# First mixer of a two-layer trunk: products of 36 rows padded to 128, mask and identity in float32r, two projections in another pair of PSUM banks

## The chip, the cores and the metric

The kernel runs on one core of a Trainium2 chip, alone. The metric is the device time of one launch in microseconds (us), the median of several runs. The profile is one more execution of the same program, taken with the hardware profiler on.

## The reference, cut to what matters

The reference is a decoder trunk of two layers for one sequence of 512 tokens and 1024 features in float32. Each layer is: half a gated feed-forward network, a mixer, another half feed-forward network, each followed by a layer norm of `alpha*x + sublayer(x)`. The mixer of the first layer has two parts side by side. One is a gated linear recurrence (RG-LRU). The other, which the change touches, is an mLSTM with four heads of width 128:

```python
qk = silu(causal_depthwise_conv(qk, conv_w, conv_b)); q, k = split(qk, 2)
log_f = log_sigmoid(if_pre[..., 4:] + f_bias)
# per head, over all earlier tokens j <= i:
#   weight(i, j) = exp(F_i - F_j + i_j - m_i),  F = cumsum(log_f), m = the running maximum
#   num_i = sum_j (q_i . k_j) weight(i, j) v_j
#   h_i   = num_i / max(|den_i|, exp(-m_i)),  den_i the same sum without v_j
```

The mixer of the second layer (RWKV-7 beside GLA) and the feed-forward networks are not edited.

## The kernel before, in words

**Products.** Activations and weights are split into two float32r parts, a high one and a low one (`xh`/`xl`, `whi`/`wlo`), and a product of the two is three TensorE matmuls: high x high, low x high, high x low (lines 128, 129 and 132, or 152 to 154, or 161 to 163). The high part of a weight is a ScalarE copy (line 99), the low part a VectorE subtraction (line 103). Weights come through two `raw` buffers by DMAs on SyncE's queue (line 87), and go into five `whi` and `wlo` buffers. `weights()` splits two chunks ahead of the one that it returns.

**Order.** The program is written as a sequence; a scheduler with a timeline of its own then sets the order on each engine, and each engine runs its instructions in that order. A small edit can therefore move instructions far from it. On TensorE an instruction that waits holds up all behind it.

**PSUM.** `psum(name, tag)` hands out the eight banks: tag A has four, B and C two each, used in turn. A bank is handed out again when its last reader is done.

**The start.** Line 46 loads the identity matrix `ident` on SyncE's queue, ahead of the four tiles of `x` and the first two weight chunks. `start()` keeps TensorE busy with seven products of zeros (line 63), then `to_xT` (line 174) transposes the first two tiles of `x` with `ident`, ScalarE and VectorE make `xh` (line 166) and `xl` (line 167) of them, and the first feed-forward products begin on the tokens 0 to 255.

**The mixer's front (function `even`, line 314).** After some small loads (`pc`, `ng`, and by lines 331 to 333 a mask of 128x256 numbers, which VectorE casts to bfloat16: an identity and a triangle of -1e30) come the gate projection `p_if` (PSUM tag B) and eight query-key projections, in the order 0, 1, 4, 5, 2, 3, 6, 7 of their tiles. The first four are made in two halves of 256 tokens. Each of the eight takes a bank of tag A; so the fifth to eighth reuse the banks of the first to fourth, once the convolution that reads a bank is done: one ScalarE activation (line 309) and three VectorE operations (line 312). `qk_tile` then applies SiLU (line 373).

**The exponents.** VectorE makes four stretches of F_i - m_i in `Rt` (lines 396 and 398), for key tiles 0 to 3 with 512, 384, 256 and 128 queries. Line 399 copies 32 rows of it to the float32r tile `Rs`, and line 400 puts the rounding rest of the four heads into its rows 32 to 35. `sel` (lines 388 and 389, from `ident`) has the columns that select a head. `pct` (line 405) transposes the per-key terms, and line 407 copies them to `cT`. Per head and key tile, `scores` then does:

- line 416: `pr`, a product over 36 rows of `sel` and `Rs` (tag B): the exponents
- line 417: the mask added to its first 128 columns, a bfloat16 product of identity and triangle
- line 419: the exponential on ScalarE into `wt`
- line 421: `pS`, query x key in plain float32 (tag B too, so `pr` and `pS` alternate on two banks)
- line 423: VectorE multiplies the two into `pT`.

There are 16 such steps. TensorE's part of them is laid among the value projection `pv` (four banks of tag A, lines 152 to 154), the recurrence's projections `prg` and `pgg`, and `po`.

Of the kernel before, what the change touches and what calls it, by code (L numbers as in the profile page):

```python
# [7 lines left out]
F32 = mybir.dt.float32  # L8
F32R = mybir.dt.float32r
BF = mybir.dt.bfloat16  # L10
AF = mybir.ActivationFunctionType
ALU = mybir.AluOpType
P = 128
# [18 lines left out]
class Net:  # L32
    def __init__(self, ctx, tc, a):
        self.tc = tc
        self.nc = nc = tc.nc
        self.a = a
        E = ctx.enter_context
        self.cp = E(tc.tile_pool(name="cp", bufs=1))
        self.wp = E(tc.tile_pool(name="wp", bufs=1))
        self.lp = E(tc.tile_pool(name="lp", bufs=1))  # L40
        self.ps = E(tc.tile_pool(name="ps", bufs=1, space=bass.MemoryType.PSUM))
        self.new_x()
        self.xh = self.cp.tile([P, 8, S], F32R, name="xh")
        self.xl = self.cp.tile([P, 8, S], F32R, name="xl")
        self.ident = self.cp.tile([P, P], F32, name="ident")
        nc.sync.dma_start(self.ident, a["c_ident"])

        self.cp.tile([P, 56], F32, name="pad")
        self.expo = self.cp.tile([P, 1], F32, name="expo")
        nc.gpsimd.memset(self.expo, -0.5)  # L50
        ctx.callback(lambda: self.xp.release())
        self.srcs = []
        self.nl = self.nsp = self.nu = 0
        self.raw = {}
        self.adds = range(0)
        self.spl = {}
# [257 lines left out]
    def even(self, l):  # L314
        nc, a, tc = self.nc, self.a, self.tc
        V, A, T, G = nc.vector, nc.scalar, nc.tensor, nc.gpsimd
        with tc.tile_pool(name="ev", bufs=1) as ep:
            bufs = dict(qk=8, row=4, wt=3, v=4, u=4, rg=6, o=6)

            def slot(tag, n=S):  # L320
                return ep.tile([P, 516 if tag == "v" else S], F32, name=tag, tag=tag, bufs=bufs[tag])[:, :n]
# [5 lines left out]
            IFB = 72  # L327
            ng = ep.tile([P, S], F32, name="ng")
            nc.sync.dma_start(ng, a["ml_norm_g"].broadcast_to([P, S]))
            msk = ep.tile([P, 2, P], BF, name="msk")  # L330
            mtmp = slot("wt", 256)
            nc.sync.dma_start(mtmp.rearrange("p (a b) -> p a b", a=2), a["c_mask_neg"])
            V.tensor_copy(out=msk, in_=mtmp.rearrange("p (a b) -> p a b", a=2))
            wbd = ep.tile([P, 8, P], F32, name="wbd")
            G.memset(wbd, 0.0)
            for i, nm in enumerate(("rg_wa", "rg_wx")):
# [11 lines left out]
            p_qk = {}  # L348
            order = (0, 1, 4, 5, 2, 3, 6, 7)
# [20 lines left out]
            def qk_tile(i):  # L370
                qk[i] = slot("qk")
                self.conv(qk[i], p_qk[i], pc, MCW + i, MCB + i, 8)
                A.activation(qk[i], qk[i], AF.Silu)
# [9 lines left out]

            Rt = ep.tile([32, 1280], F32, name="Rt")
            G.memset(Rt, 0.0)
            Rs = ep.tile([36, 1280], F32R, name="Rs")
            sel = ep.tile([36, 4], F32R, name="sel")
            A.activation(sel[0:32], self.ident[0:32, 0:4], AF.Copy)
            A.activation(sel[32:36], self.ident[32:36, 32:36], AF.Copy)
            R, off = [], 0  # L390
            for bj in range(4):
                n = S - bj * P
# [17 lines left out]
            def scores(h):  # L410
                pT = ep.tile([P, 1280], F32, name=f"pT{h}", tag="pT", bufs=4)
                out, off = [], 0
                for bj in range(4):
                    n = S - bj * P
                    pr = self.psum("pr")
                    T.matmul(pr[:, :n], sel[:, h:h + 1].broadcast_to([36, P]), R[bj], start=True, stop=False)
                    T.matmul(pr[:, :P], msk[:, 0, :], msk[:, 1, :], start=False, stop=True)
                    wt = slot("wt")
                    A.activation(wt[:, :n], pr[:, :n], AF.Exp, bias=cT[:, bj, h:h + 1])
                    pS = self.psum("pS")  # L420
                    T.matmul(pS[:, :n], qk[4 + h][:, bj * P:(bj + 1) * P], qk[h][:, bj * P:], start=True, stop=True)
                    o = pT[:, off:off + n]
                    V.scalar_tensor_tensor(out=o, in0=pS[:, :n], scalar=128 ** -0.5, in1=wt[:, :n], op0=ALU.mult, op1=ALU.mult)
                    out.append(o)
                    off += n
                return out


            for i in order[4:]:
                p_qk[i] = self.psum("pqk", "A")  # L430
                self.project_T(p_qk[i], self.weights())
                qk_tile(i)
            pT = [scores(h) for h in range(4)]

            acc = [self.psum("pv", "A") for _ in range(4)]
# [725 lines left out]
def layouts(inp):  # L1161
    import numpy as np
    c = np.ascontiguousarray
    f = np.float32
# [39 lines left out]
    pc[32:36, 72] = inp["ml_f_bias"][0]  # L1204
    o["ev_pc"] = pc
    o["c_ident"] = np.eye(P, dtype=f)
    mk = np.zeros((P, 2, P), f)
    mk[:, 0] = np.eye(P)
    mk[:, 1] = np.where(np.arange(P)[None, :] < np.arange(P)[:, None], -1e30, 0.0)
    o["c_mask_neg"] = mk  # L1210
    w = inp["od_w_in"][0]
    t = T_chunks(w[:, :1664])
# [62 lines left out]
```

## Time and profile before

| | |
|---|---|
| median of 3 runs | 2037.82 us (2034.89 to 2042.15) |
| the profiled execution's own time | 2032.82 us |
| its span, from the first to the last instruction | 2031.0 us |
| mean granted TensorE clock over the span | 0.992 |
| TensorE busy over the span | 2000.3 us (98%) |
| the mixer's stretch, 380 to 620 us: TensorE busy, granted clock | 237.22 of 240 us, 0.99 |
| the same stretch: VectorE, ScalarE | 172.54 us, 122.58 us |
| second mixer, 1340 to 1640 us: TensorE busy, granted clock | 283.52 of 300 us, 0.96 |

Rows of the timeline give the start in us from the span's start, the duration, the engine (PE is TensorE, PEld its weight loads, DVE VectorE, ACT ScalarE, POOL GpSimd, SP SyncE), the line, the operation with its tiles and shape, and in square brackets the idle time before it and what ended it. Matmuls overlap in these rows: the distance from one start to the next tells what a matmul costs, and its duration does not. A row of a tile or line gives minimum, median and maximum of the duration in ns. A row of DMA issues ends with the us from issue to landing.

### The profile page before, as it was taken

To read this page: it belongs to the slowest core of one execution; us is meant where nothing else is said; L and a number is where in the kernel's file an instruction comes from. 1 tells how busy PE (TensorE), PEld (TensorE's weight loads), DVE (VectorE), ACT (ScalarE), POOL (GpSimd) and SP (SyncE) were. 2 spreads that over 40 slices of the span, in tenths; PEclk is the share of its full clock that TensorE was granted. 3 is DMA by queue.
4 is the path that set the end of the run, shared out by engine and by line. 5 is a ranking of instruction groups with operands and counts; after the bars stand their busy time and mean duration, and the time that the engine had idled before them with its cause. 6 is when DMAs were issued, how large, how long until landed. Compare 5 with 4: busy or idle time off the path is not lost. (4 is left out here: it accounts for less than half of the span.)

```text
span 2031.0 us, 26072 instructions
## 1 busy us (share of the span) xinstructions
PE 2000.3 (98%) x10485; PEld 1660.6 (82%) x10485; DVE 959.9 (47%) x1794; ACT 722.4 (36%) x1272; POOL 101.1 (5%) x162
## 2 busy tenths in 40 slices
PE   9999999999999999999999999999999999999998
PEld 8888888976888888888988888896777788888886
DVE  4332333766784333335533333466756773323335
ACT  4332332456423322331432233158545333322330
POOL 0000000100010000000000000012122210000001
PEclk9999999999999999999999999999998999999999
DMA  5233232332223333331433333254636033333331
GB/s 178 94 96 122 94 101 86 98 93 63 73 85 114 102 94 116 102 94 57 131 94 95 115 102 97 83 163 112 142 67 173 2 97 112 101 96 115 101 96 63
DMA packets 59914, 204.02 MB, mean 100 GB/s; under 512 B 7872, under 2 KB 8336, under 8 KB 59792
## 3 DMA queue, kind: packets, MB, share of 16 engines
q1 hardware_dynamic: 56336, 189.77, 30.0%
q0 software_dynamic: 3456, 12.58, 3.4%
q8 instruction: 82, 1.34, 0.3%
q14 instruction: 40, 0.33, 0.0%
HBM read 198.13 MB, written 4.19 MB: 100 GB/s over the span
## 5 line engine op out<-in xcount | busy, mean ns | idle before, releaser
L99 ACT ACTIVATE whi<-raw 128x512 fp32r<-128x512 f32 x661 | 379.6, 623 | 818.6 <-PE pgu L129 401.7
L103 DVE TENSOR_TENSOR wlo<-raw,whi 128x512 fp32r<-128x512 f32 x610 | 395.0, 687 | 537.6 <-ACT whi L99 511.8
L128 PE MATMUL pgu<-xh,whi 128*128 128x512 f32 (+1 forms) x1568 | 563.4, 368 | 1.6 <-ACT whi L99 1.3
L129 PE MATMUL pgu<-xl,whi 128*128 128x512 f32 (+1 forms) x1568 | 564.5, 368 | 0.0
L132 PE MATMUL pgu<-xh,wlo 128*128 128x512 f32 (+1 forms) x1568 | 353.7, 368 | 0.0
L128 PEld LDWEIGHTS pgu<-xh,whi 128*128 128x128 f32 x1568 | 294.3, 189 | 50.4 <-ACT whi L99 1.5
L129 PEld LDWEIGHTS pgu<-xl,whi 128*128 128x128 f32 x1568 | 295.2, 189 | 48.6
L132 PEld LDWEIGHTS pgu<-xh,wlo 128*128 128x128 f32 x1568 | 275.8, 189 | 48.6
L161 PE MATMUL acc<-whi,hh 128*128 128x512 f32 x704 | 274.6, 390 | 0.0
L162 PE MATMUL acc<-whi,hl 128*128 128x512 f32 x704 | 274.3, 390 | 0.0
L163 PE MATMUL acc<-wlo,hh 128*128 128x512 f32 x704 | 272.5, 390 | 0.0
L239 DVE TENSOR_TENSOR sg<-sg,pgu 128x512 f32<-128x512 f32 (+1 forms) x96 | 61.7, 643 | 335.2 <-PE pgu L132 331.0
L162 PEld LDWEIGHTS acc<-whi,hl 128*128 128x128 f32 x704 | 132.2, 188 | 27.3
L163 PEld LDWEIGHTS acc<-wlo,hh 128*128 128x128 f32 x704 | 132.2, 188 | 27.2
L161 PEld LDWEIGHTS acc<-whi,hh 128*128 128x128 f32 x704 | 132.2, 188 | 27.0
L166 ACT ACTIVATE hh<-sg 128x512 fp32r<-128x512 f32 (+1 forms) x96 | 57.2, 596 | 121.2 <-DVE sg L239 121.2
L196 POOL TENSOR_SCALAR rs<-mv 128x1 f32<-128x1 f32 x24 | 13.1, 547 | 1503.0 <-DVE mv L194 1503.0
L238 ACT ACTIVATE sg<-pgu 128x512 f32<-128x512 f32 (+1 forms) x96 | 53.6, 560 | 55.7 <-PE pgu L132 55.0
L166 ACT ACTIVATE xh<-pst 128x512 fp32r<-128x512 f32 x48 | 27.6, 597 | 112.8 <-PE pst L174 112.6
L128 PE MATMUL pj<-xh,whi 128*128 128x512 f32 (+2 forms) x184 | 61.9, 356 | 0.0
L167 DVE TENSOR_TENSOR hl<-sg,hh 128x512 fp32r<-128x512 f32 (+1 forms) x96 | 61.6, 642 | 0.6 <-ACT hh L166 0.5
L129 PE MATMUL pj<-xl,whi 128*128 128x512 f32 (+2 forms) x184 | 60.5, 346 | 0.0
(346 smaller groups left out, 2006.4 us busy)
## 6 DMA issues: line engine op xcount, KB each, us to landing
raw<-ffn_wi SPq DMA_DIRECT2D x176, 512.0 KB, 3.5
raw<-ffn_wo SPq DMA_DIRECT2D x88, 512.0 KB, 3.5
raw<-od_krv SPq DMA_DIRECT2D x12, 512.0 KB, 3.8
raw<-ev_qk SPq DMA_DIRECT2D x8, 512.0 KB, 3.6
raw<-ev_rg SPq DMA_DIRECT2D x8, 512.0 KB, 3.4
raw<-ev_w_out SPq DMA_DIRECT2D x8, 512.0 KB, 3.5
raw<-od_w_out SPq DMA_DIRECT2D x8, 512.0 KB, 4.0
wlo<-od_krv POOLq DMA_DIRECT2D x6, 512.0 KB, 6.6
```

The costliest lines, as they stand in the source:

```text
L99: self.nc.scalar.activation(hi[:, sl], t[:, sl], AF.Copy)
L103: self.nc.vector.tensor_tensor(out=lo[:, sl], in0=t[:, sl], in1=hi[:, sl].bitcast(F32), op=ALU.subtract)
L128: mm(o, hi[:, kt, :n], self.xh[:, kt, t0:t1], start=kt == 0, stop=False)
L129: mm(o, hi[:, kt, :n], self.xl[:, kt, t0:t1], start=False, stop=lo is None and kt == 7)
L132: mm(o, lo[:, kt, :n], self.xh[:, kt, t0:t1], start=False, stop=kt == 7)
L161: mm(o, ah, hi[:, cs], start=first and i == 0, stop=False)
L162: mm(o, al, hi[:, cs], start=False, stop=False)
L163: mm(o, ah, lo[:, cs], start=False, stop=last and i == len(lhs) - 1)
L166: self.nc.scalar.activation(hi, src, AF.Copy)
L167: self.nc.vector.tensor_tensor(out=lo, in0=src, in1=hi.bitcast(F32), op=ALU.subtract)
L238: nc.scalar.activation(sg, pp[f, 0][:, t0:t1], AF.Silu)
L239: nc.vector.tensor_tensor(out=sg, in0=sg, in1=pp[u][:, t0:t1], op=ALU.mult)
```

## The change

Four edits, and what the scheduler makes of them.

- **Identity.** `ident` becomes a float32r tile (`identr`, read as float32 through `ident`). Its load moves from SyncE's queue to GpSimd's, ahead of the memset of `expo`.
- **Mask.** The mask keeps only its triangle, 128x128, as float32r, and the mask product takes `identr` as its other operand.
- **Rows.** `Rs` and `sel` get 128 rows. Four new ScalarE activations (scale 0 on `expo`) write zeros into their rows 32 to 127; rows 32 to 35 are then overwritten as before. The product of line 416 runs over 128 rows.
- **Banks.** The fifth and sixth query-key projections take the two banks of tag C; the seventh and eighth take the first two of tag A.

```diff
-        self.ident = self.cp.tile([P, P], F32, name="ident")
-        nc.sync.dma_start(self.ident, a["c_ident"])
+        self.identr = self.cp.tile([P, P], F32R, name="ident")
+        nc.gpsimd.dma_start(self.identr, a["c_ident"])
+        self.ident = self.identr.bitcast(F32)
...
-            msk = ep.tile([P, 2, P], BF, name="msk")
-            mtmp = slot("wt", 256)
-            nc.sync.dma_start(mtmp.rearrange("p (a b) -> p a b", a=2), a["c_mask_neg"])
-            V.tensor_copy(out=msk, in_=mtmp.rearrange("p (a b) -> p a b", a=2))
+            msk = ep.tile([P, P], F32R, name="msk")
+            mtmp = slot("wt", P)
+            nc.sync.dma_start(mtmp, a["c_mask_neg"])
+            V.tensor_copy(out=msk, in_=mtmp)
...
-            Rs = ep.tile([36, 1280], F32R, name="Rs")
-            sel = ep.tile([36, 4], F32R, name="sel")
+            Rs = ep.tile([P, 1280], F32R, name="Rs")
+            sel = ep.tile([P, 4], F32R, name="sel")
+
+            A.activation(Rs[32:64].rearrange("p (a b) -> p a b", a=10), self.expo[32:64].unsqueeze(2).broadcast_to([32, 10, P]), AF.Copy, scale=0.0)
+            A.activation(Rs[64:128].rearrange("p (a b) -> p a b", a=10), self.expo[64:128].unsqueeze(2).broadcast_to([64, 10, P]), AF.Copy, scale=0.0)
+            A.activation(sel[32:64], self.expo[32:64].broadcast_to([32, 4]), AF.Copy, scale=0.0)
+            A.activation(sel[64:128], self.expo[64:128].broadcast_to([64, 4]), AF.Copy, scale=0.0)
...
-                    T.matmul(pr[:, :n], sel[:, h:h + 1].broadcast_to([36, P]), R[bj], start=True, stop=False)
-                    T.matmul(pr[:, :P], msk[:, 0, :], msk[:, 1, :], start=False, stop=True)
+                    T.matmul(pr[:, :n], sel[:, h:h + 1].broadcast_to([P, P]), R[bj], start=True, stop=False)
+                    T.matmul(pr[:, :P], self.identr, msk, start=False, stop=True)
...
-                p_qk[i] = self.psum("pqk", "A")
+                p_qk[i] = self.psum("pqk", "C" if i in order[4:6] else "A")
```

The order that the scheduler makes differs in three stretches: the start, this mixer, and (in small ways) the second mixer. Lines of the changed kernel are up to six higher.

TensorE at the seventh query-key projection, before (`pqk_3169` is the sixth projection, `pqk_3208` the seventh):

```order
L129 MATMUL pqk_3169<-xl_72,whi_2811 128x512
L132 MATMUL pqk_3169<-xh_71,wlo_2812 128x512 x8
L405 MATMUL pct_3123<-ident_73,row_3058 128x64 x4
L128 MATMUL pqk_3208<-xh_71,whi_3131 128x512
L129 MATMUL pqk_3208<-xl_72,whi_3131 128x512
```

The same place in the changed program (`pqk_3173` is the sixth, `pqk_3212` the seventh):

```order
L133 MATMUL pqk_3173<-xh_71,wlo_2812 128x512 x8
L129 MATMUL pqk_3212<-xh_71,whi_3135 128x512
L130 MATMUL pqk_3212<-xl_72,whi_3135 128x512
...
L411 MATMUL pct_3127<-ident_73,row_3058 128x64 x4
L130 MATMUL pqk_3212<-xl_72,whi_3135 128x512
...
L133 MATMUL pqk_3212<-xh_71,wlo_3136 128x512 x8
```

The seventh projection now begins right behind the sixth, and the four small transposes have moved nine matmuls into it.

TensorE at the first exponents, before (`pv_3418` is the value projection's first tile of tokens):

```order
L132 MATMUL pqk_3247<-xh_71,wlo_3171 128x512 x8
L416 MATMUL pr_3287<-Rs_3098,sel_3099 128x512
L417 LDWEIGHTS msk_2761
L417 MATMUL pr_3287<-msk_2761 128x128
L421 MATMUL pS_3292<-qk_3067,qk_3079 128x512
L152 MATMUL pv_3418<-whi_3209,xh_71 128x512
```

And in the changed program:

```order
L133 MATMUL pqk_3251<-xh_71,wlo_3175 128x512 x8
L153 MATMUL pv_3422<-whi_3213,xh_71 128x512
L154 MATMUL pv_3422<-whi_3213,xl_72 128x512
L155 MATMUL pv_3422<-wlo_3214,xh_71 128x512
L153 MATMUL pv_3422<-whi_3213,xh_71 128x512
L422 MATMUL pr_3291<-Rs_3098,sel_3099 128x512
L423 MATMUL pr_3291<-msk_2761,ident_73 128x128
L427 MATMUL pS_3296<-qk_3067,qk_3079 128x512
```

Four matmuls of the value projection have moved ahead of the first exponents, and the mask has lost the separate weight load of its bfloat16 form.

ScalarE at the program's start, before (`pst_104` and `pst_111` are the halves of the first tile of `x`, `pst_118` and `pst_125` of the second; `whi_135` and `whi_141` the first two weight chunks):

```order
L166 ACT_TABLE_LOAD
L166 ACTIVATE xh_71<-pst_104 128x4x128
L166 ACTIVATE xh_71<-pst_111 128x4x128
L166 ACTIVATE xh_71<-pst_118 128x4x128
L166 ACTIVATE xh_71<-pst_125 128x4x128
L99 ACTIVATE whi_135<-raw_96 128x512 x2
L99 ACTIVATE whi_141<-raw_98 128x512 x2
```

And in the changed program:

```order
L167 ACT_TABLE_LOAD
L167 ACTIVATE xh_71<-pst_104 128x4x128
L167 ACTIVATE xh_71<-pst_111 128x4x128
L100 ACTIVATE whi_135<-raw_96 128x512 x2
L167 ACTIVATE xh_71<-pst_118 128x4x128
L167 ACTIVATE xh_71<-pst_125 128x4x128
L100 ACTIVATE whi_141<-raw_98 128x512 x2
```

The first weight chunk has moved ahead of the second tile of `x`. On TensorE the first feed-forward products behind the transposes now read (before, the first sixteen were all of `pgu_157` with `whi_135`):

```order
L175 MATMUL pst_125<-ident_73,x_70 128x128 x4
L129 MATMUL pgu_157<-xh_71,whi_135 128x256
L129 MATMUL pgu_166<-xh_71,whi_141 128x256
L130 MATMUL pgu_157<-xl_72,whi_135 128x256
L129 MATMUL pgu_157<-xh_71,whi_135 128x256
```

The second matmul belongs to the second weight chunk and stands ahead of all others of the first.

More of the change, by code (lines that the diff above doesn't have):

```diff
@@ L1206, in layouts @@
     o["c_ident"] = np.eye(P, dtype=f)
-    mk = np.zeros((P, 2, P), f)
-    mk[:, 0] = np.eye(P)
-    mk[:, 1] = np.where(np.arange(P)[None, :] < np.arange(P)[:, None], -1e30, 0.0)
+    mk = np.where(np.arange(P)[None, :] < np.arange(P)[:, None], f(-1e30), f(0))
     o["c_mask_neg"] = mk
```

## The prediction

> **What bounds the kernel now.** First the page, for the engine that carries the span:
>
> ```profile
> PE 2000.3 (98%) x10485; PEld 1660.6 (82%) x10485; DVE 959.9 (47%) x1794; ACT 722.4 (36%) x1272; POOL 101.1 (5%) x162
> ```
>
> TensorE is busy for 98% of 2031.0 us, so a change pays where TensorE stands still or spends more than its columns need, and time saved there is saved at the end. Next the waits of TensorE alone, in which one belongs to the change:
>
> ```profile
> PE pqk L128 <- DVE qk L312: 1.9, 1, 1.9
> ```
>
> The timeline of TensorE shows that place: four small transposes, the first matmul of the seventh projection, its ninth, its last eight in one row, and the eighth projection's first.
>
> ```profile
> 413.50 0.46 PE L405 MATMUL pct<-ident,row 64*128 64x64 f32 x4
> 415.87 0.77 PE L128 MATMUL pqk<-xh,whi 128*128 128x512 f32 x1 [1.90 <-DVE qk L312]
> ...
> 419.33 0.39 PE L128 MATMUL pqk<-xh,whi 128*128 128x512 f32 x1
> ...
> 421.17 1.98 PE L132 MATMUL pqk<-xh,wlo 128*128 128x512 f32 x8
> 422.98 0.39 PE L128 MATMUL pqk<-xh,whi 128*128 128x512 f32 x1
> ```
>
> The last eight stand (422.98 - 421.17) / 8 = 0.226 us apart, the first eight (419.33 - 415.87) / 8 = 0.433. So behind an idle time of 1.90 us TensorE runs at half pace for 3.46 us. What the seventh projection waits for is the third tile's convolution, whose bank it reuses:
>
> ```profile
> 414.99 0.73 DVE L312 SCALAR_TENSOR_TENSOR qk<-pqk,pc,qk 128x509 f32<-128x509 f32 x1
> ```
>
> It ends at 415.72. Last, the same timeline at one of the 16 score steps with 512 queries, whole, and the pair of one with 128:
>
> ```profile
> 452.10 0.39 PE L152 MATMUL pv<-whi,xh 128*128 128x512 f32 x1
> 452.41 0.50 PE L416 MATMUL pr<-Rs,sel 36*128 36x512 f32 x1
> 452.84 0.23 PE L417 MATMUL pr<-msk 128*128 128x128 bf16 x1
> 452.88 0.48 PE L153 MATMUL pv<-whi,xl 128*128 128x512 f32 x1
> 453.20 0.39 PE L154 MATMUL pv<-wlo,xh 128*128 128x512 f32 x1
> ```
>
> ```profile
> 447.35 0.32 PE L416 MATMUL pr<-Rs,sel 36*128 36x128 f32 x1
> 447.61 0.23 PE L417 MATMUL pr<-msk 128*128 128x128 bf16 x1
> ```
>
> At a pace of 0.226 us the first group would need little more than 0.226 each for `pv`, `pr` and `pv`. Ahead of the 36-row product stand 0.31 us, behind it 0.43, and the `pv` behind the mask takes 0.32. With 128 queries the distance from `pr` to the mask is 0.26: 384 columns fewer save 0.17, as columns should, and some 0.2 us remain that do not depend on them.
>
> **The banks: -3.6 us.** With the fifth and sixth projections in tag C, the seventh takes the bank of the first, read long before 413.5. From 413.50 to 422.98 lie 9.48 us; the same work without the wait and at full pace is some 0.4 us of transposes and 24 x 0.226 = 5.4, so 5.8. The saving is 3.65, of which 1.90 is the wait and 8 x (0.433 - 0.226) = 1.65 the half pace. The lower end is the wait alone, 1.9, if a usual execution has no half pace here.
>
> What is late next? The first exponents of before:
>
> ```profile
> 428.51 0.50 PE L416 MATMUL pr<-Rs,sel 36*128 36x512 f32 x1
> ```
>
> TensorE reaches them at 428.51 less 3.6, plus four `pv` that now stand ahead: near 425.8. They need `Rs`, and the exponential behind them a table:
>
> ```profile
> 421.34 1.69 DVE L400 TENSOR_TENSOR Rs<-Rt,Rs 4x512 fp32r<-4x512 f32 x4
> ```
>
> ```profile
> 429.42 1.28 ACT L419 ACT_TABLE_LOAD   x1
> 430.71 0.69 ACT L419 ACTIVATE wt<-pr,cT 128x512 f32<-128x512 f32 x1
> ```
>
> `Rs` is ready at 423.0, 2.8 us early. The second `pr` needs the bank that this exponential reads. TensorE gets there after `pr` and mask (0.35), `pS` (four passes, some 0.9) and 18 `pv` (4.1): 431.1. Even where it stands now the exponential ends at 431.4, and it should move earlier with the eighth projection. So the cover is thin but there; without it the cost is 0.3 us. Two more table loads of 1.28 stand on ScalarE now; the dearer place is the SiLU between the second and the third exponential, some 3.2 us, and TensorE has 20 `pv` and a `pS` there, over 5 us. I give them nothing.
>
> **Rows and mask: -4.5 us.** One step of 512 queries costs 453.20 - 452.10 - 2 x 0.226 = 0.65 us for `pr` and mask, one of 128 by the shorter distance 0.48; between them 0.59 and 0.53. Four of each make 9.0 us. Afterwards the product has the same row count and type as its neighbours, so `pr` should cost its columns: 0.226 and 0.17, and for the short ones what the projections with 256 columns show, 0.12:
>
> ```profile
> 401.54 1.12 PE L132 MATMUL pqk<-xh,wlo 128*128 128x256 f32 x8
> 402.50 0.40 PE L128 MATMUL pqk<-xh,whi 128*128 128x512 f32 x1
> ```
>
> Eight lie in 0.96 us. The mask, 128 columns with a fresh weight load, I take at that 0.12 too, since a shorter float32r product in full rows is not in the trace. That is 0.35, 0.29, 0.24 and 0.24, four of each: 4.5. Bounds: if a 128-column product costs 0.06 the saving is 6; if the 0.2 us behind `pr` come with the short mask and not with the rows, it is near 1. I take 4.5, since the 256-column rows are the nearest.
>
> The mask's weights are where the change gives something up:
>
> ```profile
> L417 PEld LDWEIGHTS <-msk x16: 94/96/97, 428.9 to 521.7; 128*128 128x128 bf16 x16
> ```
>
> ```profile
> L132 PEld LDWEIGHTS pqk<-xh,wlo x96: 187/192/193, 375.7 to 428.0; 128*128 128x128 f32 x96
> ```
>
> A load takes 0.19 in float32r, 0.096 in bfloat16. The eight matmuls above had such loads of 0.19 and stood 0.12 apart, so most of a load is hidden. The Trainium skill ("TensorE: Matmul & The Clock Gate", Weight-path perf modes) says that fast weight load is on for 128 weights whose type is not FP32, and that it wins where the free size is small: a rule against this change. The loads of this trace agree with it; if all of the difference showed, the sum would be 16 x 0.096 = 1.5 us worse.
>
> **The mixer's front: +0.15.** ScalarE gets two activations of 1280 columns and three short ones at 383 us.
>
> ```profile
> L399 ACT ACTIVATE Rs<-Rt x4: 293/454/612, 418.8 to 420.1; 32x512 fp32r<-32x512 f32 x1, 32x384 fp32r<-32x384 f32 x1, 32x256 fp32r<-32x256 f32 x1, 32x128 fp32r<-32x128 f32 x1
> ```
>
> ```profile
> 386.58 0.21 ACT L452 ACTIVATE tm<-pc 128x4 f32<-128x4 f32 x1 [3.05 <-DMA pc<-ev_pc]
> ```
>
> ```profile
> 388.84 0.39 PE L128 MATMUL pif<-xh,whi 128*128 128x256 f32 x1 [0.42 <-ACT xh L166]
> ```
>
> From 128 to 512 columns a copy grows by 0.32 us, so 1280 columns take 1.25 (an estimate). Two of them and two of 0.2 make 2.9, inside the 3.05 us in which ScalarE waits for `pc`. But the second `sel` copy now stands behind `tm`, ahead of the `xh` for which TensorE already waits: +0.15, bounds 0 and 0.5. The smaller mask and its cast on VectorE are hidden by the same wait; nothing waits on SyncE for the mask.
>
> **The start: +2.5.** SyncE's issues, then landings and first uses:
>
> ```profile
> 0.72 0.39 SPq L46 DMA_DIRECT2D ident<-c_ident  x1
> 1.17 0.90 SPq L65 DMA_DIRECT2D x<-x  x2
> 2.10 0.91 SPq L87 DMA_DIRECT2D raw<-ffn_wi  x2
> ```
>
> ```profile
> raw<-ffn_wi SPq DMA_DIRECT2D x1, 512.0 KB, 5.2
> ```
>
> ```profile
> 4.84 2.60 PE L174 MATMUL pst<-ident,x 128*128 128x128 f32 x16 [0.50 <-DMA x<-x]
> 8.74 0.39 PE L128 MATMUL pgu<-xh,whi 128*128 128x256 f32 x1 [1.30 <-ACT whi L99]
> 8.97 0.28 PE L129 MATMUL pgu<-xl,whi 128*128 128x256 f32 x1
> 9.09 0.28 PE L128 MATMUL pgu<-xh,whi 128*128 128x256 f32 x1
> ```
>
> ```profile
> 5.97 2.21 ACT L166 ACTIVATE xh<-pst 128x512 fp32r<-128x512 f32 x4 [3.96 <-PE pst L174]
> 8.05 2.20 ACT L99 ACTIVATE whi<-raw 128x512 fp32r<-128x512 f32 x4
> ```
>
> Without `ident` on its queue SyncE issues `x` 0.45 us earlier, and TensorE's transposes, which wait for `x`, can begin near 4.39. Whether they do hangs on `ident` from GpSimd's queue. The trace has the same 64 KB from SyncE in 1.8 us and only larger loads from GpSimd:
>
> ```profile
> wlo<-od_krv POOLq DMA_DIRECT2D x6, 512.0 KB, 6.6
> ```
>
> Between a landing at 2.5 and one past 7.3 (up to 3 us later than now) I take the first, by the size. The Trainium skill ("DMA: Bandwidth & Descriptors", Anatomy of one DMA) gives 2.0 us plus the bytes over 436 GB/s for a load from GpSimd: an estimate of 2.15, in time for `x`; no run here shows one of this size.
>
> Dearer is the new order. The second feed-forward product is now of the second weight chunk, and seven ScalarE operations of some 0.55 stand ahead of it from the first `xh` on: 3.95 us, where the stream now begins 8.74 - 5.97 = 2.77 behind it. One matmul runs ahead, so the stream is 1.06 later. Take off 0.45 for `x`; add 0.25, since the first weight chunk, landing at 2.1 + 5.2 = 7.3 or 0.45 earlier, holds up ScalarE: +0.85. And TensorE then stands idle from about 7.0 to 9.7 but for one matmul, longer than the 1.90 us behind which the mixer ran at half pace (1.30 us here left 0.12 between matmuls). I add that price, 1.65. Bounds: -0.4 (no delay of the stream) and +5.
>
> The second mixer's changed order moves ready work past ready work; no term, but a half pace more or less there is 1.65 either way.
>
> **The sum.** -3.6 - 4.5 + 0.15 + 2.5 = -5.5 us. The profiled execution took 2032.82, so it would take 2027.3. The median of the runs is 5.0 above it, so the forecast for a median is 2037.82 - 5.5 = 2032.3.
>
> **The rivals.**
>
> 1. *The start is cheap.* ScalarE keeps up or the half pace stays away: then the sum is -7 to -8.4 and the time about 2030. For: the weight chunk may not be late. Against: the order, which puts seven operations ahead. Chance 0.23.
> 2. *The rows give half.* The 0.2 us belong to the short mask, or the identity's load shows: -1 to -3 in place of -4.5, so about 2034.8. For: the loads of 0.19. Against: 0.31 us ahead of the 36-row product, where no mask stands. Chance 0.14.
> 3. *The half pace was an accident of this execution.* The banks give 1.9 only: 2034.0. For: the runs spread over 7 us. Against: the idle time was nearly two us and its end is in the rows. Chance 0.13.
> 4. *Slower: ScalarE takes over at the scores.* If the first exponential comes more than 0.3 us later than worked out, TensorE waits at the second `pr`, and at the third and fourth again, each behind a pair of table switches; three waits of 1.9 with a half pace each cost 3 x 3.55 = 10.6, so 2043. It decides where the eighth convolution is held up by a late `raw`. Chance 0.05.
>
> The forecast itself has 0.45. A measurement of this kernel can tell about 0.3%, 6.1 us, from no change. The forecast and rivals 2 and 3 lie within it, rival 1 beyond it; runs scatter by some 3 us about each. Faster by more: 0.42; within: 0.53; slower: 0.05. The range, 2026.5 to 2038, takes in rival 1 with the larger saving on the rows (2032.3 - 4 - 1.5) and rivals 2 and 3 with the scatter; it leaves out rival 4.
>
> **What would show it.** In the profile of the changed kernel: no wait and distances of 0.226 in the seventh projection; some 0.35 us for `pr` and mask of 512 columns; `pif` waiting 0.5 to 0.6; the second feed-forward product near 9.7 and distances near 0.22 for some 3 us behind it. I am wrong on the start if distances of 0.12 stand from 9 us on, on the rows if the step still costs over 0.5, on the banks if TensorE waits between 413 and 440.

## The result, and the profile after

| | before | changed |
|---|---|---|
| median of 6 runs each, us | 2037.44 (2034.52 to 2042.15) | 2048.26 (2045.96 to 2052.31) |
| ratio, 95% interval | | 1.0056 [1.0043, 1.0069] |
| profiled execution, its span | 2031.0 | 2047.2 |

The change made the kernel slower by 0.56%, some 11 us, where 5.5 us less was forecast. The ratios are worked out from the single runs, so they can differ a little from the quotient of the medians.

TensorE still carries the span, and its matmuls are as many as before. The page of the changed kernel, the line that was shown of before:

```profile
PE 2014.3 (98%) x10485; PEld 1674.5 (82%) x10485; DVE 960.1 (47%) x1794; ACT 728.2 (36%) x1278; POOL 101.6 (5%) x163
```

Of the 16 us of span 14.0 stand in this line as more busy time (2014.3 against 2000.3), for as many matmuls: they took longer. The mean granted clock of TensorE tells the same: it was 0.980 to 0.985 in the six runs of the changed kernel, and 0.988 to 0.994 in the runs of the kernel before. Neither tells where. Since both profiles hold 10485 matmuls, the k-th matmul of one can be set beside the k-th of the other. What the changed kernel gains or loses between two points of the order is then (times of before's profile):

| stretch of before, us | changed minus before, us |
|---|---|
| 0 to 44, the start | +5.7 |
| 412 to 602, the first mixer | -7.5 |
| 602 to 1361 | 0.0 |
| 1361 to 1395 | +4.3 |
| 1412 to 1451 | +4.9 |
| 1566 to 1591 | +11.2 |
| 1591 to 1664 | -1.2 |
| the rest | -1.2 |

The first mixer gained nearly what was forecast. The start lost more than twice as much as forecast, and the second mixer, which no edit touches, lost 18 us by this one pair of profiles.

**The first mixer.** The timeline of TensorE in the changed kernel, at the end of the sixth projection, the start of the seventh, and one step with 512 queries:

```profile
411.69 1.98 PE L133 MATMUL pqk<-xh,wlo 128*128 128x512 f32 x8
413.51 0.39 PE L129 MATMUL pqk<-xh,whi 128*128 128x512 f32 x1
413.73 0.39 PE L130 MATMUL pqk<-xl,whi 128*128 128x512 f32 x1
...
421.08 0.46 PE L411 MATMUL pct<-ident,row 64*128 64x64 f32 x4
```

```profile
451.77 0.40 PE L154 MATMUL pv<-whi,xl 128*128 128x512 f32 x1
452.00 0.39 PE L422 MATMUL pr<-Rs,sel 128*128 128x512 f32 x1
452.24 0.22 PE L423 MATMUL pr<-msk,ident 128*128 128x128 f32 x1
452.29 0.45 PE L155 MATMUL pv<-wlo,xh 128*128 128x512 f32 x1
452.58 0.40 PE L153 MATMUL pv<-whi,xh 128*128 128x512 f32 x1
```

The wait of 1.90 us and the half pace behind it are gone. The step now costs 452.58 - 451.77 - 2 x 0.226 = 0.36 us, where it cost 0.65.

**The start.** The timeline of TensorE, with the wait for the identity, then the first products; and the DMA view of the first 12 us of both kernels (last number: us from issue to landing), the changed one first:

```profile
6.92 3.67 PE L175 MATMUL pst<-ident,x 128*128 128x128 f32 x16 [2.57 <-DMA ident<-c_ident]
11.10 0.58 PE L129 MATMUL pgu<-xh,whi 128*128 128x256 f32 x1 [0.51 <-ACT xh L167]
12.10 0.58 PE L129 MATMUL pgu<-xh,whi 128*128 128x256 f32 x1 [0.42 <-ACT whi L100]
12.48 0.41 PE L130 MATMUL pgu<-xl,whi 128*128 128x256 f32 x1
12.70 0.41 PE L129 MATMUL pgu<-xh,whi 128*128 128x256 f32 x1
```

```profile
ident<-c_ident POOLq DMA_DIRECT2D x1, 64.0 KB, 5.7
```

```profile
ident<-c_ident SPq DMA_DIRECT2D x1, 64.0 KB, 1.8
```

The 64 KB landed at 6.92 us instead of 2.5, so the transposes began 2.08 later, and the 16 of them took 3.67 us instead of 2.60. The second product came at 12.10 instead of 8.97, and the stream then ran at 0.21 us per matmul, half pace, until 15.7 us.

**The second mixer.** The windows view of 1576 to 1612 us, before and changed. The columns are the stretch, its length, the busy time of TensorE, weight loads, VectorE, ScalarE and GpSimd, then the granted TensorE clock, the DMA share and GB/s:

```profile
1576.00:1612.00 36.00, 33.85 (x304) 25.30 (x305) 26.88 (x103) 13.52 (x36) 10.30 (x24) 1.00 0.01 1
```

```profile
1576.00:1612.00 36.00, 33.67 (x246) 24.11 (x245) 18.61 (x66) 6.44 (x17) 5.06 (x12) 0.67 0.06 12
```

TensorE is busy for nearly the same time in both; the granted clock is 1.00 in one and 0.67 in the other, and 246 matmuls fit instead of 304. The reader should look at the clock column here, since the busy column hides the loss. VectorE's timeline shows what stands in front of it. Before:

```profile
1573.80 0.49 DVE L862 TENSOR_TENSOR St<-St,Dm 128x128 f32<-128x128 f32 x2
1575.02 0.41 DVE L851 TENSOR_TENSOR KV<-psa,ZU 64x256 f32<-64x256 f32 x1 [0.72 <-PE psa L850]
...
1576.41 0.68 DVE L1040 TENSOR_TENSOR kr<-kr,og 128x512 f32<-128x512 f32 x1
```

Changed:

```profile
1579.91 0.51 DVE L868 TENSOR_TENSOR St<-St,Dm 128x128 f32<-128x128 f32 x2
1581.91 0.69 DVE L1046 TENSOR_TENSOR kr<-kr,og 128x512 f32<-128x512 f32 x1 [1.50 <-ACT kr L899]
1582.52 0.41 DVE L857 TENSOR_TENSOR KV<-psa,ZU 64x256 f32<-64x256 f32 x1
```

And TensorE in the changed kernel, behind it:

```profile
1581.01 0.65 PE L1022 MATMUL pkv<-kr,kn 64*64 64x128 f32 x8
1582.99 1.22 PE L863 MATMUL pst<-KV,BK 128*128 128x128 f32 x4 [1.32 <-DVE KV L857]
```

The scheduler has put the product of `yg` and `og` (tile `kr`) ahead of `KV`. Its operand comes from ScalarE, whose `kr` ends at 1576.09 in the profile of before:

```profile
1574.59 1.50 ACT L893 ACTIVATE kr<-po,sm 128x128 f32<-128x128 f32 x4 [2.76 <-POOL sm L891]
```

With `KV` ready, TensorE's `pst` had gone on without a wait there:

```profile
1575.49 0.71 PE L857 MATMUL pst<-KV,BK 128*128 128x128 f32 x4
```

In the changed kernel VectorE stands 1.50 us at work that isn't ready, `KV` stands behind it, and TensorE's `pst` waits 1.32 us for `KV`. The four matmuls of `pst` then take 1.22 us where they took 0.71, and half pace lasts for 23.9 us. That wait alone does not tell the loss. TensorE waits for `KV` three times in either kernel, and in all for as long. The waits of TensorE, before and changed (us in total, times, longest):

```profile
PE pst L857 <- DVE KV L851: 2.3, 3, 0.9
```

```profile
PE pst L863 <- DVE KV L857: 2.2, 3, 1.3
```

What differs is where they fall. The granted clock changes only at the ends of steps of 3.413 us (last section). In the changed kernel a wait of 0.93 us for `St` and the first 0.7 us of the wait for `KV` fall into one step, 1578.96 to 1582.37; TensorE is busy for 1.77 us of it, and half pace begins at its end. In before the step with the wait for `St`, 1572.92 to 1576.33, has 2.42 us of busy time, and full pace goes on.

The waits of the changed kernel show a second place, near 1428 us:

```profile
PE pa L699 <- DVE y L746: 1.5, 1, 1.5
```

Here VectorE makes `y` at 1422.84 in before and at 1427.53 in the changed kernel. In both, four operations stand ahead of it, on `wk`, `KRV`, `wk` and `bk`; the first of them needs `pi`, a transpose on TensorE. Before, `pi` on TensorE, then the last of the four and `y` on VectorE:

```profile
1413.60 0.60 PE L728 MATMUL pi<-ident,wk 128*128 128x128 f32 x4
```

```profile
1417.81 0.69 DVE L733 SCALAR_TENSOR_TENSOR bk<-wk 128x512 f32<-128x512 f32 x1
...
1422.84 0.69 DVE L740 TENSOR_TENSOR y<-kr,pb 128x512 f32<-128x512 f32 x1
```

Changed, `pi`, then the first and the last of the four and `y`:

```profile
1420.13 0.60 PE L734 MATMUL pi<-ident,wk 128*128 128x128 f32 x4
```

```profile
1422.79 0.75 DVE L736 SCALAR_TENSOR_TENSOR wk<-kr,pc,pi 128x512 f32<-128x512 f32 x1
...
1425.63 0.69 DVE L739 SCALAR_TENSOR_TENSOR bk<-wk 128x512 f32<-128x512 f32 x1
...
1427.53 0.69 DVE L746 TENSOR_TENSOR y<-kr,pb 128x512 f32<-128x512 f32 x1
```

The four were done by 1418.50 and now run up to 1426.3, with three short operations between them and `y`. What moved first is TensorE's `pi`: it stands 20 matmuls later in the order.

### The profile page after: what moved, and what is told of

It is laid out like the page before. It is cut to its first block, busy times and chain, and to the rows that moved or that the text cites. A ratio compares the mean times of both kernels' runs of the same rounds, so it can differ in the third digit from the quotient of the medians.

```text
span 2047.2 us, 26077 instructions
## 1 busy us (share of the span) xinstructions
PE 2014.3 (98%) x10485; PEld 1674.5 (82%) x10485; DVE 960.1 (47%) x1794; ACT 728.2 (36%) x1278; POOL 101.6 (5%) x163
## 4 chain that ended last, share of the span: by engine, by line
PE 90%; DVE 4%; ACT 3%; DMA 2%; issue 1%; POOL 0%; POOLq 0%; DVEq 0%; ACTq 0%; SPq 0%
PE pgu L129 16%; PE pgu L130 16%; PE pgu L133 16%; PE acc L162 8%; PE acc L163 8%; PE acc L164 8%; PE pout L164 1%; PE pout L162 1%; PE pout L163 1%; PE pj L129 1%; PE pj L130 1%; PE pj L133 1%; PE pv L153 1%; PE pst L175 1%; PE pv L154 1%
## 5 line engine op out<-in xcount | busy, mean ns | idle before, releaser
L164 PEld LDWEIGHTS acc<-wlo,hh 128*128 128x128 f32 x704 | 132.2, 188 | 27.3
```

Of the source, the lines that this page charges most:

```text
L164: mm(o, ah, lo[:, cs], start=False, stop=last and i == len(lhs) - 1)
```

## The experiments

Theory A: the loss in the second mixer is made by the new order at these two places, whatever edit brought the scheduler to it. Its sharper form C: it is made by what VectorE's instructions there wait for and hold up. Rival B: TensorE reaches the second mixer at another time, and that costs. Rival D: TensorE's own changed order, or the clock by itself, makes the half pace. Rival E: the edits themselves do it. The names of the stretches below are the times of before's first profile, as in the table above. The expectations call the second place "`y` behind `bk`"; by the rows above `bk` stands ahead of `y` in both kernels, and it is `pi`, with the four behind it, that moved.

### 1. Rows and mask alone

```diff
+        self.identr = self.cp.tile([P, P], F32R, name="identr")
...
+            V.tensor_copy(out=self.identr, in_=self.ident)
```

These lines stand in place of the identity's edit, with `ident` left on SyncE's queue in float32; the edits of rows and mask are as in the change, the banks as before.

> The 128 rows and the float32r mask alone: the identity stays on SyncE's queue in float32 and VectorE copies it once to a float32r tile; the fifth and sixth projections stay in tag A. The order of the start and of the second mixer is that of before. Theory A (the loss of the changed kernel sits in the new order of the second mixer, whatever brings it): 2037.4 less the 3.7 us by which the changed kernel runs ahead over the scores, 2033.7, and the second mixer has before's three half-pace stretches, 24 us in all. Theory B (the loss is one of time: TensorE reaches the second mixer earlier than its partners, or falls otherwise on the clock's windows; the order does not matter): TensorE is 3.7 us early there as in the changed kernel (2.0), so most of the 18 us comes here too, 2040 to 2052.

Measured: 2034.38, ratio 0.9985 [0.9973, 0.9997]. In its profile the first mixer gains 4.0 us, and from 1412 to 1591 it is 0.8 shorter in all. The start is 3.0 longer, though its order on TensorE is that of before, and the 1361 stretch costs 3.6 with no row of TensorE's order changed there, which A did not expect. A has the time, and this stretch needed a look of its own (experiment 8).

### 2. The identity's queue alone

```diff
-        nc.sync.dma_start(self.ident, a["c_ident"])
+        nc.gpsimd.dma_start(self.ident, a["c_ident"])
```

> Only the load of the identity moves from SyncE's to GpSimd's queue (still float32); first mixer as before. The scheduler answers with the start and the second mixer of the changed kernel. Theory A (order): +5.7 at the start and +18 in the second mixer, 2061, with long half-pace stretches near 1380, 1430 and 1590 us. Theory B (time): TensorE is 5.7 us late there, not early, so the second mixer keeps before's 24 us of half pace: 2043.

Measured: 2049.92, ratio 1.0071 [1.0047, 1.0095]: 11 us below A and 7 above B. Start +4.3, 1412 stretch +3.3, 1566 stretch +6.7, 1361 stretch -0.1. The places are those of A; A's 18 us came from a pair of profiles and are too many for a median. The seven runs spread from 2041.70 to 2058.91, at granted clocks of 0.991 to 0.981, and the profile is of one of the shortest. In it `pst` waits 1.31 us for `KV` as in the changed kernel, but this wait and the one for `St` fall into two steps of the clock, with TensorE busy for 2.10 and 2.40 of 3.41 us; half pace begins only at 1591.38 and lasts 10.2 us instead of 23.9. What the same wait costs thus hangs on where the steps fall in that execution.

### 3. The banks alone

```diff
-                p_qk[i] = self.psum("pqk", "A")
+                p_qk[i] = self.psum("pqk", "C" if i in order[4:6] else "A")
```

> Only the fifth and sixth projections in tag C. The start is that of before; the second mixer gets nearly the changed kernel's order. Theory A (order): -4.0 from the banks and +18 in the second mixer, 2051. Theory B (time): TensorE is 4 us early at the second mixer, which costs some of the 18 us whatever the order; it cannot tell itself from A here unless the time is near 2033, which refutes both.

Measured: 2050.83, ratio 1.0062 [1.0047, 1.0076], as A has it. The first mixer gains 3.5, the second loses 4.9 and 11.1 at the two places. One line that saves 3.5 us thus costs 13 in all.

### 4. The whole change without the identity's queue

The edits of experiment 1 with the banks.

> The whole change but for the identity's queue: it is loaded on SyncE's queue in float32 and copied on VectorE to a float32r tile. The start is that of before; in the second mixer the rows of TensorE near 1373 us keep before's order and those from 1560 us on have the changed one. Theory A (order): -4.0 -3.7 from the first mixer, nothing at 1380, up to 12 us from 1580 on: 2030 to 2041. Theory B (time): the same first mixer and TensorE 7.7 us early at the second, the loss there at least as large as in the changed kernel: 2047 or more.

Measured: 2044.48, ratio 1.0030 [1.0015, 1.0045]: 3.5 us above A's range and 2.5 below B's. Its 1412 stretch, where the scheduler left `pi` and the four, costs 0.3; its 1566 stretch, with the product ahead of `KV`, costs 12.5. The 1361 and the 1481 stretch cost 4.7 and 3.0 here, but the kernel before can lose nearly as much there (experiment 8), so the excess over A stays open. Two of the twelve runs took 2033.80 and 2036.31 at granted clocks of 0.991 and 0.989, the others 2041.68 or more at 0.982 to 0.986: the order brings the loss in most executions, not in all.

### 5. The changed kernel with the product on GpSimd

```diff
-                    V.tensor_tensor(out=yg[t], in0=yg[t], in1=og[t], op=ALU.mult)
+                    G.tensor_tensor(out=yg[t], in0=yg[t], in1=og[t], op=ALU.mult)
```

> The changed kernel with one edit in the second mixer: the product of `yg` and `og` (line 1046) is made on GpSimd instead of VectorE. TensorE's rows near 1580 us keep the changed order. Theory C (in the changed order VectorE stands at this product, waiting 1.50 us for ScalarE's `kr`, with `KV` behind it, and TensorE's `pst` waits 1.32 us for `KV`; the half pace of 23.9 us follows from that wait): VectorE no longer stands there, the wait of `pst` is below 0.5, the long half-pace stretch goes and with it some 11 us: 2037. Theory D (the changed order of TensorE's own small matmuls near 1580, or the clock, makes the half pace): the stretch stays and the time is 2048.

Measured: 2036.93, ratio 1.0000 [0.9988, 1.0012]. One line, four instructions moved off VectorE, gives back 11.3 us of the changed kernel's median. VectorE, TensorE and the window of its profile:

```profile
1582.37 0.42 DVE L857 TENSOR_TENSOR KV<-psa,ZU 64x256 f32<-64x256 f32 x1 [0.71 <-PE psa L856]
```

```profile
PE pst L863 <- DVE KV L857: 1.1, 2, 0.5
```

```profile
1576.00:1612.00 36.00, 32.78 (x317) 23.97 (x316) 27.56 (x106) 11.97 (x31) 15.05 (x28) 1.00 0.09 16
```

`KV` again follows `psa`, the longest wait of `pst` falls from 1.3 to 0.5, and the clock is 1.00. TensorE's rows there kept the changed order, so D falls for this place.

### 6. Experiment 4 with the product on GpSimd

> The whole change but for the identity's queue (loaded on SyncE's queue in float32, copied on VectorE), with the product of `yg` and `og` on GpSimd. Theory C: the kernel without the GpSimd load took 2044.5; its long half-pace stretch from 1577 us (27.3 us, some 11 us lost) goes: 2033, below the time before. Theory D: the stretch stays: 2044.

Measured: 2035.08, ratio 0.9992 [0.9975, 1.0008], 2 us above what C had. The long stretch is gone from its profile, but 6.8 us of half pace stand at 1589 us and the 1566 stretch still costs 3.9. What brought that is open; no such row of VectorE stands ahead of it. One of the twelve runs took 2050.22 at a granted clock of 0.982, so a loss of that size is not ruled out here.

### 7. Everything but the banks

The change as it is, with all eight projections in tag A. The scheduler leaves `KV` ahead of the product.

> The whole change but for the banks: all eight projections in tag A, the identity on GpSimd's queue, 128 rows and float32r mask. The start has the changed order, and the second mixer near 1580 us the order of before (VectorE makes `KV` ahead of the product of `yg` and `og`). Theory C: no long half pace from 1580 on; 2037.4 + 4 to 6 for the start - 3.7 for rows and mask = 2038 to 2040. Theory D in the form that the clock does it by chance of time: 2045 to 2052, with the stretch of 24 us.

Measured: 2040.41, ratio 1.0013 [1.0003, 1.0023]. The 1566 stretch costs 0.0 and the start 4.8, as C has it; the time is 0.4 above C's range. With experiment 1 it gives a price for the identity's queue, 2040.41 - 2034.38 = 6 us, but not one of the start alone: of the 7.5 us between the two profiles 1.8 lie at the start and 4.3 from 1591 to 1664, where TensorE waits 5.6 us for a load instead of 2.8.

### 8. The kernel before, once more

> The kernel before, once more, for a second profile of the same program. The first profile (2032.8, below all but one of its timed runs) had half pace in 27 us, none of it at the start or near 1380 us. If the half pace at those two places is a matter of the execution and not of the order, this one may show either of them, at about 3 us each, with no row of the order changed; the stretch from 1580 on must be absent, since its order is not there.

Measured: one time, 2040.57, and a profile with the same program. Against the first profile of before it is longer by 1.3 at the start, 3.7 from 1361 to 1395 and 3.0 from 1481 to 1511, and shorter by 2.5 from 1591 on; at the two places of A it differs by 0.2 and 0.0. The windows view of 1376 to 1396, first profile and second:

```profile
1376.00:1396.00 20.00, 17.97 (x96) 12.51 (x96) 12.27 (x21) 13.70 (x25) 5.65 (x6) 1.00 0.56 135
```

```profile
1376.00:1396.00 20.00, 18.88 (x82) 12.82 (x81) 10.39 (x17) 12.93 (x24) 5.26 (x5) 0.83 0.55 128
```

The same order at the same place runs at 1.00 in one execution and at 0.83 in another. So the 1361 and the 1481 stretch belong to the execution. Of the 16 us between the profiles of before and changed, the 4.3 of the 1361 stretch are of this sort: the first profile of before was a lucky one, 4.6 us below its median.

### 9 and 10. The kernel before with nine and with five products of zeros

The plainest test: no edit near any mixer, only the count of warm-up products at the start, chosen because the scheduler answers with both new places (nine) or with the one near 1428 alone (five).

```diff
-        for _ in range(7):
+        for _ in range(9):
```

> The kernel before with nine products of zeros at the start instead of seven; nothing else is edited. The scheduler answers with the changed kernel's order in the second mixer, at both places: the product of `yg` and `og` ahead of `KV` on VectorE (near 1580 us) and `y` behind `bk` (near 1428 us). Theory C: `pst` waits 1.3 us and `pa` 1.5 us for VectorE, long half pace from 1580 us; 2037.4 + 11 + 4 and up to 0.5 for the start: 2052. Theory E (the second mixer's loss comes from the first mixer's edits or from the identity's load themselves): 2038.

Measured: 2053.35, ratio 1.0076 [1.0055, 1.0097]. VectorE, TensorE and the clock of this kernel:

```profile
1585.95 0.69 DVE L1040 TENSOR_TENSOR kr<-kr,og 128x512 f32<-128x512 f32 x1 [1.50 <-ACT kr L893]
1586.56 0.41 DVE L851 TENSOR_TENSOR KV<-psa,ZU 64x256 f32<-64x256 f32 x1
```

```profile
1587.03 1.22 PE L857 MATMUL pst<-KV,BK 128*128 128x128 f32 x4 [1.31 <-DVE KV L851]
```

```profile
1576.00:1612.00 36.00, 33.57 (x272) 24.32 (x269) 17.57 (x61) 6.60 (x17) 5.84 (x13) 0.64 0.14 30
```

The wait, its size and the half pace are those of the changed kernel, without any of its edits. E falls. B falls too: this kernel comes to the second mixer 3.2 us late and loses 13.0 in the 1566 stretch, while the kernel of experiment 12 comes 5.2 early and loses nothing there. Over all profiles, the five with the product ahead of `KV` on VectorE come 7.1 early to 4.2 late and lose 6.7 to 13.0; the six others of experiments that keep `KV` first come 5.2 early to 3.7 late and lose nothing.

> The kernel before with five products of zeros at the start. The scheduler changes the second mixer's order at one place alone, near 1428 us (`y` behind `bk` on VectorE); near 1580 us it stays. Theory C: `pa` waits 1.5 us for `y` with half pace behind it, `pst` waits at most 0.9 for `KV`: 2037.4 + 4 = 2041. The shorter run of zeros can add up to 2 us of half pace at the start (to 2043). Theory E: 2038 to 2040, without the wait of `pa`.

Measured: 2042.23, ratio 1.0022 [1.0008, 1.0036]; 1566 stretch 0.0, 1412 stretch +1.8, start +1.8. `pa` waits 1.0 us for `y`, less than expected, and no half pace lies behind it. The place near 1428 is worth 2 to 5 us: 1.8 in this kernel, 3.3 in two others with one step of half pace behind the wait, 4.9 to 5.0 in four with two. In all seven `pi` stands 20 matmuls later on TensorE, in the others it does not. No run moved one instruction of this place by itself, so its mechanism is argued from the rows and not shown as that near 1580 is.

### 11. The identity on ScalarE's queue

```diff
-        nc.sync.dma_start(self.ident, a["c_ident"])
+        nc.scalar.dma_start(self.ident, a["c_ident"])
```

> The kernel before with the load of the identity moved to ScalarE's queue, which like SyncE's is a hardware one; the order of ScalarE at the start and the second mixer near 1428 and 1580 us stay as before. If the loss at the start of the changed kernel (4 to 6 us) comes from the late landing on GpSimd's queue (TensorE waited 2.6 us for it) and from the order that the scheduler made for it, there is none here, and `x` is issued 0.45 us earlier: 2036 to 2038. If it comes from any move of this load off SyncE's queue: 2041 to 2043.

Measured: 2037.31, ratio 1.0000 [0.9985, 1.0016]. The time has it, the reason only in part: the load is late here as well, in the DMA view of the first 12 us:

```profile
ident<-c_ident ACTq DMA_DIRECT2D x1, 64.0 KB, 4.2
```

It lands at 4.9, with `x` under way at the same time, but `x` lands then too. The start of this profile is 3.2 us longer, where none was expected. On SyncE's queue it went ahead of `x` and took 1.8.

### 12. All edits of the first mixer in an order that leaves `KV` alone

Rows, mask and banks, the identity on ScalarE's queue with a copy on VectorE, five products of zeros.

> All edits of the first mixer (128 rows, float32r mask, banks), the identity on ScalarE's queue in float32 with a copy on VectorE, and five products of zeros: the scheduler then leaves the second mixer's order near 1580 us as it was; the place near 1428 us is changed. Theory C: -3.8 (banks) -3.6 (rows and mask) + 4 at 1428 us: 2034, with no long half pace from 1580 us. Theory E: 2045 or more, as in the kernel that differs only in the queue and the zeros (2044.5).

Measured: 2033.72, ratio 0.9984 [0.9971, 0.9997]; 1566 stretch 0.0, first mixer -7.2. This beats both kernels, as does experiment 1; both are some 0.15% below before.

## Why the prediction was wrong, step by step

- **The banks, -3.6: right.** 3.5 us in experiment 3. Rival 3 (the half pace there an accident): nearly always false. Of the eight profiles with all projections in tag A, seven have 3.4 us of half pace behind the wait, that of experiment 7 has none, and its first mixer gains 1.4 more than that of experiment 1. The wait of 1.9 us is there in experiment 7 as well, but it falls across two steps of the clock.
- **Rows and mask, -4.5: a little too much.** 4.0 by the profile of experiment 1, 3.0 by its median. The step of 512 costs 0.36 where 0.35 was worked out. The weight load of the mask does take twice as long now, as the first row of the view by line shows:

```profile
L423 PEld LDWEIGHTS pr<-msk,ident x16: 187/188/188, 431.4 to 520.8; 128*128 128x128 f32 x16
```

  In the step `pr` takes 0.24 and mask with load some 0.12, the price that was taken for them. By its 128 columns alone the mask would cost half of what 256 columns do, 0.06 (an estimate), so up to 0.06 per step, 1 us in all, can be the slower load. The rule of the Trainium skill on fast weight load ("TensorE: Matmul & The Clock Gate", Weight-path perf modes) agrees with the loads; what it is worth here no run separates. Nor does any run separate the 128 rows from the float32r mask: experiment 1 makes both edits, so which of them gives the 0.3 us per step is open.
- **The mixer's front, +0.15: not there; the cover of the first exponents: right.** From 378 to 412 us the changed kernel differs by -0.2, where two profiles of the kernel before differ by 0.5, and `pif` waits 0.3 us where 0.5 to 0.6 was forecast. TensorE waits for no exponent.
- **The start, +2.5: mis-sized.** Between a landing of the identity at 2.5 and one past 7.3 the prediction took the first, "by the size". It landed at 6.92. The Trainium skill's fit for a load from GpSimd ("DMA: Bandwidth & Descriptors", Anatomy of one DMA) gave an estimate of 2.15 us; measured were 5.7 from issue to landing, beside transfers of 512 KB on another queue. The half pace behind it came as forecast, 0.21 us per matmul. Four profiles with this load lose 3.6 to 5.7 at the start against the first profile of before, 4.6 on the mean; the nine others lose -0.3 to 3.2, 1.6 on the mean. So some 3.0 belong to the load and the order that goes with it. (Seven operations of 0.55 are 3.85, where the prediction has 3.95; that is a tenth of a us.)
- **The second mixer, "moves ready work past ready work; no term": the step that failed.** Near 1580 us a product whose operand was not ready moved ahead of `KV` on VectorE, and TensorE's next step hangs on `KV`. The rows to see it were there: ScalarE's `kr` ends at 1576.09, `KV` began at 1575.02 and TensorE's `pst` at 1575.49. With the product in front, `KV` cannot begin before 1576.09 + 0.6, so `pst` waits over a microsecond. The price of the half pace was wrong as well: 1.65 was taken, one stretch behind a wait among large matmuls; among the small matmuls of the second mixer it lasted 23.9 us and cost ten. The changed kernel against experiment 5 puts the place at 11.3 us. Near 1428 us `pi` moved back on TensorE, and work that had been done 4 us ahead of `y` came to stand just ahead of it; seven profiles put this place at 1.8 to 5.0, 4.0 on the mean.
- **Rival 4, slower through ScalarE at the scores: the right side, the wrong mechanism.** TensorE's only wait at the scores is one of 0.5 us for `pT`.
- **The sum.** With -3.5, -4.0, +3.0 for the start, +4.0 and +11.3 the median of before gives 2037.4 + 10.8 = 2048.2; 2048.3 was measured. That it comes so near is luck: the terms come in part from single profiles, and experiment 8 shows a stretch of the same program to differ by up to 3.7 us between two executions. The lower end of the range, worked out as 2032.3 - 4 - 1.5, is 2026.8 and not 2026.5; nothing hangs on it.

## What to carry to other kernels

Where a scheduler makes the order, every edit has a second effect that can be larger than its own: here two products of zeros more at the start cost 16 us, nearly all of it around 1430 and 1580 us, and one line put on another engine gave 11 back. Compare the orders of all engines over the whole program, and for each instruction that moved ahead of another ask whether its operands are ready by the profile of before and who waits for what it now holds up; for each that moved back, as `pi` did, ask where the work that needs it now falls. Then price the wait with the pace that follows it, and take two profiles of the same program before a difference between two of them is explained.

## What the runs showed of the hardware that was not expected

- **Half pace comes in steps of 3.413 us on a fixed grid.** In the trace's record of the granted clock of each of these 14 profiles all stretches at half clock within the span's work begin at whole multiples of 3.413 us from the first one and last 1 to 8 such steps (3.4, 6.8, 10.2, 23.9 and 27.3 us among them). The Trainium skill ("TensorE: Matmul & The Clock Gate", Part 1) speaks of a free-running window of about 3.4 us, which agrees; where the grid falls on the work differs from execution to execution, as experiment 8 shows at 1376 us. The Trainium skill also gives there an idle window of that length as the condition for half pace; that part does not agree, since none of the steps in question was idle throughout. Ahead of the seven stretches behind the wait of the seventh projection TensorE was busy for 1.5 to 1.6 us of a step, ahead of the four long stretches near 1580 for 1.8 to 2.1. In experiment 7 the same wait of 1.9 us fell across two steps with 1.9 and 3.0 us of busy time, and no half pace followed.
- **The busy time of TensorE does not tell the pace.** From 1576 to 1612 it is 33.67 us at a clock of 0.67 and 33.85 at 1.00. Full pace did not come back for seven steps, while matmuls of at most 128 columns ran. What the clock goes by in such work is open, and the busy time of a step does not settle it: 2.10 us brought no half pace right behind it in experiment 2, 2.11 did in experiment 4. Nothing here measured it by itself.
- **A load of 64 KB took 1.8, 4.2 or 5.0 to 5.7 us**, by whether it went ahead of the loads of `x` on their queue or beside them on ScalarE's or GpSimd's.
- **The record of the clock begins late.** In the changed kernel it starts when half pace ends, 15.7 us into the span; the windows view shows a clock of 1.00 from 0 to 50 us, though matmuls 0.21 us apart stand in the timeline.
